# A hybrid decoder trunk on one core: GLA and HGRN2 level factors moved off GpSimd, HGRN2's diagonal computed as a score product, and a quarter's score products issued as one group

## The chip, the cores and the metric

The kernel runs on one core of one Trainium2 chip. The metric is device time in microseconds, lower is better. Before the change three runs gave 1830.06, 1832.36 and 1833.24 us, so the median is 1832.36 us.

## The reference, cut to what matters

One layer, 1024 tokens, model width 1024. The input is normalised and modulated, and one projection of 11416 columns (`w_in`) feeds four token mixers that work side by side: A (RWKV-7), B (GLA), C (mLSTM) and D (HGRN2). Their outputs are gated, projected again (`w_branch`), merged with sigmoid gates, passed through `w_out`, added to the input and normalised.

GLA and HGRN2 are the same recurrence. With q, k, a log decay per channel and v, in chunks:

```python
b = jnp.cumsum(gc, axis=2)
rel = jnp.where(causal[:, :, None], b[:, :, :, None, :] - b[:, :, None, :, :], -jnp.inf)
attn = jnp.einsum('bhik,bhjk,bhijk->bhij', qc, kc, jnp.exp(rel))
o = attn @ vc + jnp.einsum('bhik,bhkv->bhiv', qc * jnp.exp(b), state)
```

The exponent is the sum of the log decays between the key's token j and the query's token i. It is zero for j = i, so the diagonal of `attn` is the plain product of q and k of one token ("own key"). GLA has 4 heads of 64 key channels (two heads share 128 partitions: two "pairs"), HGRN2 4 heads of 128.

## The kernel before, in words

The work has four stretches. `make_u` forms the normalised input (to about 110 us). Pass A does the eight RWKV-7 heads (to about 700 us). The second pass runs eight units in the order d0, b0, d1, c0, d2, b1, d3, c1 (d is HGRN2, b is GLA, c is mLSTM), to about 1530 us. `merge` and `finish` do the rest.

Each unit is worked in four **quarters** of 256 tokens, two chunks of 128 each. `units` writes down: a quarter of this unit, then a share of the next unit's projections, then some projections of the merge gates (table `GB`). A projection (`project`, `mm3`, lines 314 to 316) splits fp32 weights into a high and a low part and does 24 matmuls of 128x512 per half of the tokens, into a `pj` bank. Its weights come by DMA into the one buffer `wraw` (SP queue), ScalarE casts them to `whi` (line 303), VectorE forms `wlo` (line 304).

The program text is not the order on the engines. The framework's planner fixes each engine's order when the kernel is built: among the instructions that are ready by its own cost estimates it takes the one of highest priority, which is the order of the text unless a block raises it. So the projections written behind a quarter fill the places on TensorE where that quarter's products would wait. On the chip each engine then follows its list strictly, and waits where an input is late.

A quarter of HGRN2 (`d_quarter`) or GLA (`b_quarter`) splits each chunk's causal matrix by **levels** s = 64, 32, 16, 8, 4, 2, 1 (`LV`): at level s a token in the right half of a block of 2s looks at the keys in the left half. `level_factor` gives for each level a tile `x` (tag `lx`) of exponentials of the distance to the middle of the block; VectorE multiplies its right halves by q (line 973) and its left halves by k (line 975), and TensorE multiplies the two (line 989 for HGRN2, line 1143 for GLA). For s = 32 to 2 the difference to the middle is taken on GpSimd (lines 860 and 865, tile `le`) and ScalarE takes the exponential (lines 862, 863 and 866). For s = 64 ScalarE does it alone (lines 855 and 856), with the middle as a bias column.

HGRN2's score products have 64 output rows, so they use half of TensorE's columns (128*64 in the profile); the two halves r = 1 and 0 alternate. There are 26 of them in a quarter, each recorded as two passes (52). Two more products (line 991) sum q times k, which GpSimd formed (`dg`, line 968), over the channels: the own-key terms. VectorE copies the valid blocks of the scores through masks (line 1000, COPY_PREDICATED) into `AT`, whose other places stay zero, and the own-key sums into `dq` (line 1001). TensorE forms `AT` by V plus `qe` by the state (lines 1006 and 1007) into a `yw` bank for each chunk, and VectorE adds `dq` times V and writes `O` to SBUF (line 1008). `rms_out` squares `O` on ScalarE (line 877), takes the root on GpSimd (lines 878 and 879), scales on VectorE (line 880), and its tail transposes the result through a `yw` bank and sends it to DRAM.

PSUM has two banks each for `pj`, `iv`, `sc` and `yw`. Two `AT` tiles serve HGRN2 and GLA in turn. SBUF tiles of a quarter come from a pool of 20 (`h260`).

```python
for li, s in enumerate(self.LV):
    for c in range(2):
        lhs = k if s == 1 else Z[li]
...
        for r in (1, 0) if s < 64 else (0,):
```

Of the kernel before, what the change touches and what calls it, by code (L numbers as in the profile page):

```python
# [9 lines left out]
F32 = mybir.dt.float32  # L10
F32R = mybir.dt.float32r
U32 = mybir.dt.uint32
# [6 lines left out]
P = 128  # L19
# [16 lines left out]
class Hybrid:  # L36
# [759 lines left out]
    def d_consts(self):  # L796
        nc, cp = self.nc, self.cp
        self.mres = {}
        for n in (32, 64, 128):
            m = cp.tile([P, QT], F32, name=f"mres{n}")  # L800
            nc.gpsimd.memset(m[:], 1.0)
            nc.gpsimd.memset(m[:, 0:QT:n], 0.0)
            self.mres[n] = m
        self.AT = []
        for b in range(2):
            t = cp.tile([P, 2, P], F32, name=f"AT{b}")
            nc.gpsimd.memset(t[:], 0.0)
            self.AT.append(t)
        self.atn = 0

        lb = self.prow["lb"]
        l = self.PT[:, lb : lb + 4]
        e = cp.tile([P, 4], F32, name="lbe")
        nc.vector.tensor_tensor(e[:], l, l, ALU.subtract)
        nc.scalar.activation(e[:], e[:], AF.Exp)
        r = cp.tile([P, 4], F32, name="lbr")
        nc.vector.reciprocal(r[:], e[:])
        nc.vector.tensor_tensor(e[:], e[:], r[:], ALU.mult)
        self.lb = cp.tile([P, 4], F32, name="lbt")
        nc.vector.tensor_tensor(self.lb[:], e[:], e[:], ALU.subtract)  # L820
        self.omlb = cp.tile([P, 4], F32, name="omlb")
        nc.vector.tensor_scalar(self.omlb[:], self.lb[:], -1.0, 1.0, ALU.mult, ALU.add)
# [18 lines left out]
    def level_factor(self, s, cs, lg):  # L841
# [10 lines left out]
        if s == 64:  # L852
# [4 lines left out]
            return x  # L857
        ref = sp(c)[:, :, 0, s - 1 : s].broadcast_to([P, nb, s])
        e = self.h("le")
        nc.gpsimd.tensor_tensor(sp(e)[:, :, 0, :], ref, sp(c)[:, :, 0, :], ALU.subtract)  # L860
        if s == 32:
            nc.scalar.activation(sp(x)[:, :, 0, :], sp(e)[:, :, 0, :], AF.Exp)
            nc.scalar.activation(sp(x)[:, :, 1, :], sp(c)[:, :, 1, :], AF.Exp)
        else:
            nc.gpsimd.tensor_tensor(sp(e)[:, :, 1, :], sp(c)[:, :, 1, :], ref, ALU.subtract)  # L865
            nc.scalar.activation(x[:, :QT], e[:, :QT], AF.Exp)  # L866
        return x
# [89 lines left out]
    def d_quarter(self, hd, qi, q, k, lg, v, sz, S):  # L957
# [8 lines left out]
        nc.vector.tensor_tensor(qe[:, :QT], qe[:, :QT], q, ALU.mult)  # L966
        dg = self.h("dg")
        nc.gpsimd.tensor_tensor(dg[:, :QT], q, k, ALU.mult)
        Z = []
# [8 lines left out]
        for c in range(2):  # L978
            cs_ = slice(c * P, (c + 1) * P)
            nc.tensor.matmul(ps_[:, cs_], lhsT=kT[:, cs_], rhs=V[:, cs_], start=True, stop=True)  # L980
        sc2 = [self.sc() for _ in range(2)]
        for li, s in enumerate(self.LV):
            for c in range(2):
                lhs = k if s == 1 else Z[li]
                rhs = Z[li][:, c * P : (c + 1) * P].rearrange("p (b z t) -> p b z t", z=2, t=s)[:, :, 1, :]

                for r in (1, 0) if s < 64 else (0,):
                    o = sc2[c][64 * r : 64 * r + 64, 64 * li : 64 * li + 64].rearrange("p (b t) -> p b t", t=s)
                    nc.tensor.matmul(o, lhsT=lhs[:, c * P + 64 * r : c * P + 64 * r + 64], rhs=rhs, start=True, stop=True)  # L989
        for c in range(2):  # L990
            nc.tensor.matmul(sc2[c][:, 448:449], lhsT=dg[:, c * P : (c + 1) * P], rhs=self.one[:], start=True, stop=True)
        AT = self.AT[self.atn % 2]
        self.atn += 1
        dq = self.sm.tile([P, 2], F32, tag="dq", bufs=4, name=self.nm("dq"))
        for c in range(2):
            for li, s in enumerate(self.LV):
# [3 lines left out]
                nc.vector.copy_predicated(o, m, sc2[c][pr, 64 * li : 64 * li + 64].rearrange("p (b t) -> p b t", t=s))  # L1000
            nc.vector.tensor_copy(dq[:, c : c + 1], sc2[c][:, 448:449])
        O = self.h("O")
        for c in range(2):
            cc = slice(c * P, (c + 1) * P)
            po = self.yw()
            nc.tensor.matmul(po[:, 0:P], lhsT=AT[:, c, :], rhs=V[:, cc], start=True, stop=False)
            nc.tensor.matmul(po[:, 0:P], lhsT=qe[:, cc], rhs=S[:], start=False, stop=True)
            nc.vector.scalar_tensor_tensor(O[:, cc], V[:, cc], dq[:, c : c + 1], po[:, 0:P], ALU.mult, ALU.add)
            Sn = self.sm.tile([P, P], F32, tag="dS", bufs=4, name=self.nm("dS"))
# [95 lines left out]
    def b_quarter(self, pr, qi, q, k, lg, v, sz):  # L1105
# [32 lines left out]
        for c in range(2):  # L1138
# [6 lines left out]
            nc.tensor.matmul(sc[1][:, 384:386], lhsT=dg[:, cc], rhs=self.bo2[:], start=True, stop=True)  # L1145
            AT = self.AT[self.atn % 2]
            self.atn += 1
            for li, s in enumerate(self.LV):
# [103 lines left out]
    def c_unit(self, pr):  # L1252
# [25 lines left out]
        def quarter(q):  # L1278
# [10 lines left out]
            c(C_MZ + 2 * pr * P, self.silu_ev("z0", R)), c(C_MZ + (2 * pr + 1) * P, self.silu_ev("z1", R)),  # L1289
        ], quarter  # L1290

    def units(self, names):
# [311 lines left out]
```

## Time and profile before

| | |
|---|---|
| median of 3 runs | 1832.36 us |
| the profiled execution | 1833.73 us, its span 1831.9 us |
| TensorE busy | 1729.2 us, 94% of the span |
| VectorE / ScalarE / GpSimd busy | 64% / 39% / 24% |
| granted TensorE clock, mean | 0.984 |

Busy time of TensorE counts overlapping matmuls once and includes the time in which a matmul only drains, so 94% does not say that it works at its peak. "PE" is TensorE's matmul, "PEld" its weight load, DVE is VectorE, ACT ScalarE, POOL GpSimd. In a group's line the numbers behind the first bar are the total busy time in us and the mean duration of one in ns; behind the second bar stands the idle time of the engine just before them, with what ended it.

### The profile page before, as it was taken

The numbers are of one execution on the slowest core, as the hardware profiler recorded it, in microseconds if no ns is written. First come the engines' busy times: TensorE is split into PE (matmuls) and PEld (weight loads), VectorE is DVE, ScalarE is ACT, GpSimd is POOL, SyncE is SP. The second block draws the span as 40 slices with busy tenths as digits, with TensorE's granted clock in tenths as the row PEclk, the third lists the DMA queues.
The fourth block names the chain that finished last, engine by engine and source line by source line (L and its number), as shares of the span: only waits on it lengthen the run. The fifth ranks groups of instructions, "written<-read, shape, count | busy, mean of one in ns | idle before, by whom it ended". The sixth has DMA issues, their size and how long they took to land. (4 is left out here: it accounts for less than half of the span.)

```text
span 1831.9 us, 28809 instructions
## 1 busy us (share of the span) xinstructions
PE 1729.2 (94%) x10515; PEld 1364.8 (75%) x10515; DVE 1179.8 (64%) x3125; ACT 719.4 (39%) x1612; POOL 438.1 (24%) x785
## 2 busy tenths in 40 slices
PE   5989999999999999999999999999989999999998
PEld 4766777777777777777677777777667788777786
DVE  8657867668667645666877545666887654565632
ACT  5643333333333356346333353536343343222221
POOL 4721121112111121121221202221231220175410
PEclk7989999999999999999999999999999999999999
DMA  9221222223222211111121221111112125666422
GB/s 299 56 68 42 54 81 56 55 65 77 49 68 56 70 49 47 58 52 44 50 58 53 64 57 53 59 53 38 56 35 66 43 82 176 208 202 203 150 85 81
DMA packets 224278, 147.30 MB, mean 80 GB/s; under 512 B 60511, under 2 KB 203018, under 8 KB 224138
## 3 DMA queue, kind: packets, MB, share of 16 engines
q1 hardware_dynamic: 208800, 109.23, 21.9%
q10 hardware_dynamic: 15338, 36.24, 5.6%
q8 instruction: 83, 1.36, 0.3%
q14 instruction: 57, 0.47, 0.1%
HBM read 111.88 MB, written 33.56 MB: 79 GB/s over the span
## 5 line engine op out<-in xcount | busy, mean ns | idle before, releaser
L314 PE MATMUL pj<-uh,whi 128*128 128x512 f32 x1344 | 548.0, 408 | 5.0 <-DVE rn L534 3.6
L316 PE MATMUL pj<-uh,wlo 128*128 128x512 f32 x1344 | 542.3, 404 | 0.0
L315 PE MATMUL pj<-ul,whi 128*128 128x512 f32 x1344 | 539.7, 402 | 0.0
L314 PEld LDWEIGHTS pj<-uh,whi 128*128 128x128 f32 x1344 | 254.8, 190 | 54.0 <-issue 7.0
L316 PEld LDWEIGHTS pj<-uh,wlo 128*128 128x128 f32 x1344 | 254.3, 189 | 49.1 <-issue 2.4
L315 PEld LDWEIGHTS pj<-ul,whi 128*128 128x128 f32 x1344 | 254.7, 190 | 45.6 <-issue 0.9
L303 ACT CAST whi<-wraw 128x1024 fp32r<-128x1024 f32 x89 | 93.0, 1045 | 235.3 <-PE pj L315 164.3
L304 DVE TENSOR_TENSOR wlo<-wraw,whi 128x1024 fp32r<-128x1024 f32 (+1 forms) x88 | 107.9, 1226 | 62.3 <-ACT whi L303 57.8
L860 POOL TENSOR_TENSOR le<-c 128x128 f32<-128x128 f32 x120 | 56.6, 480 | 266.5 <-DVE c L826 233.1
L670 DVE TENSOR_TENSOR tm<-nb,xr 32x1 f32<-32x1 f32 (+14 forms) x240 | 71.3, 297 | 6.2 <-DMA nb<-nd 0.5
L878 POOL TENSOR_SCALAR ss<-ss 128x2 f32<-128x2 f32 x48 | 15.6, 326 | 231.7 <-ACT on L877 229.9
L535 POOL TENSOR_TENSOR rn<-rn,nhalf 128x4 f32<-128x4 f32 x16 | 19.6, 1222 | 186.7 <-DVE rn L534 171.3
L1398 ACT ACTIVATE g<-pj 128x512 f32<-128x512 f32 x64 | 37.9, 593 | 64.7 <-PE pj L316 57.6
L887 DVE SCALAR_TENSOR_TENSOR y<-yw,DV,z 128x256 f32<-128x256 f32 x48 | 22.1, 480 | 57.7 <-PE yw L885 56.7
L1457 POOL TENSOR_TENSOR acc<-acc,g 128x512 f32<-128x512 f32 x32 | 46.8, 1477 | 50.2 <-DVE g L1455 50.2
L672 DVE TENSOR_REDUCE xr<-tm 32x1 f32<-32x1 f32 (+14 forms) x240 | 54.0, 225 | 6.5
L314 PE MATMUL iv<-yt,whi 128*128 128x512 f32 x128 | 50.4, 398 | 7.8 <-ACT yt L1410 4.8
L877 ACT ACTIVATE on<-O 128x128 f32<-128x128 f32 x64 | 19.8, 310 | 93.0 <-DVE O L1163 54.3
L745 DVE SCALAR_TENSOR_TENSOR Gbd<-Gbd,fa,yw 64x64 f32<-64x64 f32 x128 | 35.8, 279 | 27.9 <-PE yw L732 25.8
L989 PEld LDWEIGHTS sc<-lx 128*64 128x64 f32 x704 | 29.5, 137 | 30.9 <-issue 13.0
L314 PE MATMUL pj<-yt,whi 128*128 128x512 f32 x128 | 50.3, 393 | 1.8 <-DVE g L1455 1.8
L866 ACT ACTIVATE lx<-le 128x256 f32<-128x256 f32 x96 | 39.7, 416 | 28.1 <-POOL le L865 27.9
(482 smaller groups left out, 3564.3 us busy)
## 6 DMA issues: line engine op xcount, KB each, us to landing
wraw<-in_w_in_dram SPq DMA_DIRECT2D x89, 512.0 KB
gdram<-g ACTq DMA_DIRECT2D x64, 256.0 KB
th<-gdram ACTq DMA_DIRECT2D x32, 512.0 KB
adaw<-in_ada_w_dram SPq DMA_DIRECT2D x16, 512.0 KB
ydram<-y SPq DMA_DIRECT2D x64, 128.0 KB
wraw<-in_w_branch_dram SPq DMA_DIRECT2D x16, 512.0 KB
yr<-ydram SPq DMA_DIRECT2D x32, 256.0 KB
x<-in_x_dram SPq DMA_DIRECT2D x8, 512.0 KB
```

Of the source, the lines that this page charges most:

```text
L303: nc.scalar.copy(hi[:, :nk, :width], raw[:, :nk, :width])
L304: eng.tensor_tensor(lo[:, :nk, :width], raw[:, :nk, :width], hi[:, :nk, :width].bitcast(F32), ALU.subtract)
L314: nc.tensor.matmul(ps[:width, :], lhsT=a, rhs=xh[:, k, :], start=k == 0, stop=False)
L315: nc.tensor.matmul(ps[:width, :], lhsT=a, rhs=xl[:, k, :], start=False, stop=False)
L316: nc.tensor.matmul(ps[:width, :], lhsT=b, rhs=xh[:, k, :], start=False, stop=k == nk - 1)
L670: nc.vector.tensor_tensor(t2, n2[:, 0:i, i].unsqueeze(1).broadcast_to([32, i, i]), x2[:, 0:i, 0:i].rearrange("p j l -> p l j"), ALU.mult)
L672: nc.vector.reduce_sum(x2[:, i, 0:i], t2, axis=AX.X)
L745: nc.vector.scalar_tensor_tensor(Gn[hr, hr], Gc[hr, hr], fa[hr, c : c + 1], yw[hr, P + 64 * h : P + 64 * h + 64], ALU.mult, ALU.add)
L860: nc.gpsimd.tensor_tensor(sp(e)[:, :, 0, :], ref, sp(c)[:, :, 0, :], ALU.subtract)
L866: nc.scalar.activation(x[:, :QT], e[:, :QT], AF.Exp)
L1398: nc.scalar.activation(g[:], ps[:], AF.Tanh, scale=0.5)
L1457: nc.gpsimd.tensor_tensor(a, a, g[:], ALU.add)
```

## The change

1. `level_factor`, used by GLA and HGRN2 (24 quarters): for s = 32 ScalarE takes four exponentials of 32 columns with the middle as bias, and one of the right halves; for s = 16 to 2 VectorE subtracts the middle from all 256 columns, and ScalarE takes the absolute value and then the exponential of its negative. GpSimd has no part in it any more.
2. `d_quarter`: `dg`, its two products and `dq` go. Instead k by q is formed as a 128x128 product for each chunk into a `yw` bank (`pd`), and VectorE copies its diagonal through the identity as a mask into `AT`. As the own-key terms are then inside `AT`, the sum for `O` is complete in PSUM; both chunks go into one `yw` bank, which `rms_out` reads.
3. The 26 score products go to a new helper `together`: it raises their priority, issues the first one (now s = 1, the levels are in reverse order), and puts the others behind it in TensorE's order.
4. HGRN2 and GLA get an `AT` pair each.

```diff
@@ -801,11 +801,13 @@
             nc.gpsimd.memset(m[:], 1.0)
             nc.gpsimd.memset(m[:, 0:QT:n], 0.0)
             self.mres[n] = m
-        self.AT = []
-        for b in range(2):
-            t = cp.tile([P, 2, P], F32, name=f"AT{b}")
-            nc.gpsimd.memset(t[:], 0.0)
-            self.AT.append(t)
+        self.AT = {}
+        for u in "db":
+            self.AT[u] = []
+            for b in range(2):
+                t = cp.tile([P, 2, P], F32, name=f"AT{u}{b}")
+                nc.gpsimd.memset(t[:], 0.0)
+                self.AT[u].append(t)
         self.atn = 0
 
         lb = self.prow["lb"]
@@ -855,15 +857,17 @@
                 nc.scalar.activation(x[:, o : o + s], c[:, o : o + s], AF.Exp, scale=-1.0, bias=c[:, o + s - 1 : o + s])
             nc.scalar.activation(sp(x)[:, :, 1, :], sp(c)[:, :, 1, :], AF.Exp)
             return x
-        ref = sp(c)[:, :, 0, s - 1 : s].broadcast_to([P, nb, s])
-        e = self.h("le")
-        nc.gpsimd.tensor_tensor(sp(e)[:, :, 0, :], ref, sp(c)[:, :, 0, :], ALU.subtract)
         if s == 32:
-            nc.scalar.activation(sp(x)[:, :, 0, :], sp(e)[:, :, 0, :], AF.Exp)
+            for b in range(nb):
+                o = 2 * s * b
+                nc.scalar.activation(x[:, o : o + s], c[:, o : o + s], AF.Exp, scale=-1.0, bias=c[:, o + s - 1 : o + s])
             nc.scalar.activation(sp(x)[:, :, 1, :], sp(c)[:, :, 1, :], AF.Exp)
-        else:
-            nc.gpsimd.tensor_tensor(sp(e)[:, :, 1, :], sp(c)[:, :, 1, :], ref, ALU.subtract)
-            nc.scalar.activation(x[:, :QT], e[:, :QT], AF.Exp)
+            return x
+
+        blk = lambda t: t[:, :QT].rearrange("p (b t) -> p b t", t=2 * s)
+        nc.vector.tensor_tensor(blk(x), blk(c), blk(c)[:, :, s - 1 : s].broadcast_to([P, nb, 2 * s]), ALU.subtract)
+        nc.scalar.activation(x[:, :QT], x[:, :QT], AF.Abs)
+        nc.scalar.activation(x[:, :QT], x[:, :QT], AF.Exp, scale=-1.0)
         return x
 
     def rms_out(self, m, q, ct, O, sz, g, eps):
@@ -964,8 +968,6 @@
         qe = self.h("qe")
         nc.scalar.activation(qe[:, :QT], c128[:, :QT], AF.Exp)
         nc.vector.tensor_tensor(qe[:, :QT], qe[:, :QT], q, ALU.mult)
-        dg = self.h("dg")
-        nc.gpsimd.tensor_tensor(dg[:, :QT], q, k, ALU.mult)
         Z = []
         for s in self.LV:
             x = self.level_factor(s, cs, lg)
@@ -978,34 +980,37 @@
         for c in range(2):
             cs_ = slice(c * P, (c + 1) * P)
             nc.tensor.matmul(ps_[:, cs_], lhsT=kT[:, cs_], rhs=V[:, cs_], start=True, stop=True)
+
+        pd = self.yw()
+        for c in range(2):
+            cs_ = slice(c * P, (c + 1) * P)
+            nc.tensor.matmul(pd[:, cs_], lhsT=k[:, cs_], rhs=q[:, cs_], start=True, stop=True)
         sc2 = [self.sc() for _ in range(2)]
-        for li, s in enumerate(self.LV):
-            for c in range(2):
-                lhs = k if s == 1 else Z[li]
-                rhs = Z[li][:, c * P : (c + 1) * P].rearrange("p (b z t) -> p b z t", z=2, t=s)[:, :, 1, :]
-
-                for r in (1, 0) if s < 64 else (0,):
-                    o = sc2[c][64 * r : 64 * r + 64, 64 * li : 64 * li + 64].rearrange("p (b t) -> p b t", t=s)
-                    nc.tensor.matmul(o, lhsT=lhs[:, c * P + 64 * r : c * P + 64 * r + 64], rhs=rhs, start=True, stop=True)
-        for c in range(2):
-            nc.tensor.matmul(sc2[c][:, 448:449], lhsT=dg[:, c * P : (c + 1) * P], rhs=self.one[:], start=True, stop=True)
-        AT = self.AT[self.atn % 2]
+
+        def level(li, s, c, r):
+            lhs = k if s == 1 else Z[li]
+            rhs = Z[li][:, c * P : (c + 1) * P].rearrange("p (b z t) -> p b z t", z=2, t=s)[:, :, 1, :]
+            o = sc2[c][64 * r : 64 * r + 64, 64 * li : 64 * li + 64].rearrange("p (b t) -> p b t", t=s)
+            return nc.tensor.matmul(o, lhsT=lhs[:, c * P + 64 * r : c * P + 64 * r + 64], rhs=rhs, start=True, stop=True)
+
+
+        todo = [(li, s, c, r) for li, s in reversed(list(enumerate(self.LV))) for c in range(2) for r in ((1, 0) if s < 64 else (0,))]
+        self.together([lambda t=t: level(*t) for t in todo])
+        AT = self.AT["d"][self.atn % 2]
         self.atn += 1
-        dq = self.sm.tile([P, 2], F32, tag="dq", bufs=4, name=self.nm("dq"))
+        nc.vector.copy_predicated(AT[:], self.ident[:].bitcast(U32).unsqueeze(1).broadcast_to([P, 2, P]),
+                                  pd[:, 0:QT].rearrange("p (c t) -> p c t", t=P))
         for c in range(2):
             for li, s in enumerate(self.LV):
                 pr = slice(0, P if s < 64 else 64)
                 o = AT[pr, c, :].rearrange("p (b z t) -> p b z t", z=2, t=s)[:, :, 1, :]
                 m = self.pmL[s][pr].bitcast(U32).rearrange("p (b t) -> p b t", t=s)
                 nc.vector.copy_predicated(o, m, sc2[c][pr, 64 * li : 64 * li + 64].rearrange("p (b t) -> p b t", t=s))
-            nc.vector.tensor_copy(dq[:, c : c + 1], sc2[c][:, 448:449])
-        O = self.h("O")
+        O = self.yw()
         for c in range(2):
             cc = slice(c * P, (c + 1) * P)
-            po = self.yw()
-            nc.tensor.matmul(po[:, 0:P], lhsT=AT[:, c, :], rhs=V[:, cc], start=True, stop=False)
-            nc.tensor.matmul(po[:, 0:P], lhsT=qe[:, cc], rhs=S[:], start=False, stop=True)
-            nc.vector.scalar_tensor_tensor(O[:, cc], V[:, cc], dq[:, c : c + 1], po[:, 0:P], ALU.mult, ALU.add)
+            nc.tensor.matmul(O[:, cc], lhsT=AT[:, c, :], rhs=V[:, cc], start=True, stop=False)
+            nc.tensor.matmul(O[:, cc], lhsT=qe[:, cc], rhs=S[:], start=False, stop=True)
             Sn = self.sm.tile([P, P], F32, tag="dS", bufs=4, name=self.nm("dS"))
             nc.vector.scalar_tensor_tensor(Sn[:], S[:], f[:, c : c + 1], ps_[:, cc], ALU.mult, ALU.add)
             S = Sn
@@ -1143,8 +1148,7 @@
                 nc.tensor.matmul(sc[li // 4][:, P * (li % 4) : P * (li % 4) + P], lhsT=lhs,
                                  rhs=R[li][:, c].rearrange("p h t -> p (h t)"), start=True, stop=True)
             nc.tensor.matmul(sc[1][:, 384:386], lhsT=dg[:, cc], rhs=self.bo2[:], start=True, stop=True)
-            AT = self.AT[self.atn % 2]
-            self.atn += 1
+            AT = self.AT["b"][c]
             for li, s in enumerate(self.LV):
                 o = AT[:].rearrange("p c (b z t) -> p c b z t", z=2, t=s)[:, :, :, 1, :]
                 m = self.pmL[s][:].bitcast(U32).rearrange("p (b t) -> p b t", t=s).unsqueeze(1).broadcast_to([P, 2, 64 // s, s])
@@ -1288,6 +1292,14 @@
             c(C_MV + 2 * pr * P, self.qcopy("v0", R)), c(C_MV + (2 * pr + 1) * P, self.qcopy("v1", R)),
             c(C_MZ + 2 * pr * P, self.silu_ev("z0", R)), c(C_MZ + (2 * pr + 1) * P, self.silu_ev("z1", R)),
         ], quarter
+
+    def together(self, fs):
+
+        with self.tc.high_priority():
+            first = fs[0]()
+            with self.tc.issue_after(first.ins):
+                for f in fs[1:]:
+                    f()
 
     def units(self, names):
```

## Rows read from the trace of the kernel before

**Rows 1.** The profile page: its first line.

```profile
span 1831.9 us, 28809 instructions
```

**Rows 2.** A stretch: us, busy PE, PEld, DVE, ACT, POOL (x), PEclk, DMA share, GB/s.

```profile
700.00:1530.00 830.00, 784.65 (x4511) 620.78 (x4510) 552.34 (x1576) 354.85 (x906) 179.26 (x364) 0.99 0.19 55
```

**Rows 3.** TensorE's timeline in the last HGRN2 quarter: start, us, engine, line, tiles, count, idle.

```profile
1438.17 0.39 PE L316 MATMUL pj<-uh,wlo 128*128 128x512 f32 x1
...
1439.89 0.49 PE L314 MATMUL pj<-uh,whi 128*128 128x512 f32 x1
...
1441.66 0.51 PE L315 MATMUL pj<-ul,whi 128*128 128x512 f32 x1
...
1442.95 0.61 PE L991 MATMUL sc<-one,dg 128*128 128x1 f32 x4
1443.41 0.48 PE L316 MATMUL pj<-uh,wlo 128*128 128x512 f32 x1
1443.73 0.39 PE L314 MATMUL pj<-uh,whi 128*128 128x512 f32 x1
1443.96 0.40 PE L315 MATMUL pj<-ul,whi 128*128 128x512 f32 x1
```

**Rows 4.** The same timeline in the second HGRN2 quarter.

```profile
757.41 0.50 PE L315 MATMUL pj<-ul,whi 128*128 128x512 f32 x1
757.85 0.69 PE L989 MATMUL sc<-lx 128*64 128x64 f32 x16
758.46 0.50 PE L316 MATMUL pj<-uh,wlo 128*128 128x512 f32 x1
```

**Rows 5.** TensorE's groups, 700 to 1530 us: count | busy, mean ns | idle before.

```profile
L989 PE MATMUL sc<-lx 128*64 128x64 f32 x704 | 39.4, 231 | 9.7 <-DVE lx L975 8.0 <-ACT lx L866 0.3
L1143 PE MATMUL sc<-Zr,lx 128*128 128x128 f32 x192 | 35.3, 293 | 8.1 <-DVE lx L1134 6.3
```

**Rows 6.** GpSimd's groups, 700 to 1530 us.

```profile
L860 POOL TENSOR_TENSOR le<-c 128x128 f32<-128x128 f32 x120 | 56.6, 480 | 266.5 <-DVE c L826 233.1 <-PE iv L917 15.5 <-issue 14.1
L865 POOL TENSOR_TENSOR le<-c 128x128 f32<-128x128 f32 x96 | 47.4, 494 | 0.0
```

**Rows 7.** VectorE's timeline in the last HGRN2 quarter: start, us, instruction.

```profile
1438.94 0.51 DVE L975 TENSOR_TENSOR lx<-lx,dk 128x128 f32<-128x128 f32 x1
1439.38 0.48 DVE L973 TENSOR_TENSOR lx<-lx,q 128x128 f32<-128x128 f32 x1
...
1441.26 0.28 DVE L975 TENSOR_TENSOR lx<-lx,dk 128x128 f32<-128x128 f32 x1
1441.47 0.30 DVE L973 TENSOR_TENSOR lx<-lx,q 128x128 f32<-128x128 f32 x1
...
1449.24 0.43 DVE L880 TENSOR_TENSOR on<-O,ss 128x256 f32<-128x256 f32 x1 [1.53 <-POOL ss L879]
```

**Rows 8.** VectorE's groups from 700 to 1530 us.

```profile
L973 DVE TENSOR_TENSOR lx<-lx,q 128x128 f32<-128x128 f32 x112 | 41.6, 372 | 2.2 <-ACT lx L866 2.1
L975 DVE TENSOR_TENSOR lx<-lx,dk 128x128 f32<-128x128 f32 x96 | 38.7, 403 | 0.0
...
L1152 DVE COPY_PREDICATED AT<-pmL,sc 128x128 f32<-128x128 uint32 x112 | 36.3, 337 | 3.0 <-PE sc L1145 0.9
...
L1008 DVE SCALAR_TENSOR_TENSOR O<-V,dq,yw 128x128 f32<-128x128 f32 x32 | 11.1, 348 | 19.1 <-PE yw L1007 17.5
...
L838 DVE TENSOR_TENSOR kt<-kt,dk 128x256 f32<-128x256 f32 x16 | 6.8, 422 | 3.7 <-ACT kt L835 3.5
```

**Rows 9.** ScalarE's groups, 700 to 1530 us.

```profile
L866 ACT ACTIVATE lx<-le 128x256 f32<-128x256 f32 x96 | 39.7, 416 | 28.1 <-POOL le L865 27.9
...
L855 ACT ACTIVATE lx<-c 128x64 f32<-128x64 f32 x48 | 13.8, 338 | 0.6 <-DVE c L826 0.6
```

**Rows 10.** The waits view of the whole span: total us, times, longest us.

```profile
ACT whi L303 <- PE pj L315: 164.3, 54, 5.6
```

**Rows 11.** The weight loads from 700 to 1530 us.

```profile
L989 PEld LDWEIGHTS sc<-lx 128*64 128x64 f32 x704 | 29.5, 137 | 30.9 <-issue 13.0 <-DVE lx L975 7.0 <-ACT lx L863 4.8
```

## The prediction

> **What bounds the kernel now.** The first line of the page gives the span, 1831.9 us [rows 1]. I then cut the span into stretches. Every line that the change touches runs in the second pass, 700 to 1530 us, and there TensorE is busy 784.65 of 830 us, while VectorE has 552, ScalarE 355 and GpSimd 179 us of work [rows 2]. TensorE's order is fixed when the kernel is built, so the end moves by what a stretch of that order gets shorter or longer, and work of another engine counts only where TensorE waits for it. The later stretches follow behind in the same order, so a microsecond won here should reach the end.
>
> Busy time hides how well TensorE is used, so I went to its timeline. Projection matmuls follow each other every 0.23 us, although each is shown 0.39 to 0.40 us long (1443.73 to 1443.96) [rows 3]: what an item costs TensorE is the distance to the next start, not its duration. In the last HGRN2 quarter the score products lie in pieces among projections. From 1438.17 to 1443.73 are 5.56 us, in which four projection matmuls start [rows 3]. They are worth 4 x 0.23 = 0.92, so the scores with the two own-key products cost 4.64 us. Read in this way the sixteen quarters cost 3.1 to 4.8 us, 4.4 on average (of them the last one's rows are shown), 70 us in all.
>
> **Tying the score products together.** A piece in the second quarter shows the price without any wait: from 757.41 to 758.46 there is one projection matmul and 16 passes, 1.05 - 0.23 = 0.82 us [rows 4]. The 16 passes span 0.69 us and one takes 0.23 on average [rows 5], so they start (0.69 - 0.23) / 15 = 0.031 us apart and need 0.47. The remaining 0.35 is the change from 128*128 to 128*64 and back, and the projection after it is late by another 0.32 - 0.23 = 0.09, as at 1443.41 [rows 3]. So a piece pays 0.44 us besides its passes. One run of 52 passes should cost 51 x 0.031 + 0.44 = 2.0 us.
>
> The own-key part: the old products take 0.46 us (1442.95 to 1443.41) [rows 3]. In place of four passes of one column there are four of 128 columns, in the form of the projections. Bounds: nothing more than now, or four whole durations of the nearest row, 4 x 0.293 = 1.17 us [rows 5], which is 0.7 a quarter and 11 us in all. I take 0.5, since matmuls of one form overlap as the projections do. That makes 2.5 us a quarter without a wait, against 4.4: a gain of 1.9 x 16 = 30 us.
>
> Now the wait. The run starts with the factor that is made last (s = 1), so it waits once for everything. Today all pieces together wait 9.7 us, 0.6 a quarter, nearly all for line 975 [rows 5]. Bounds for the new wait: nothing, or today's 0.6 plus what the chain of factors gets longer (next part, 1 us), 1.6. I take 0.6, the measured one, since it is the same engine and the same lag behind the planner's order. The gain becomes (4.4 - 2.5 - 0.6) x 16 = 21 us. Behind the waiting run stand only the projections of the next unit, and ScalarE's and VectorE's copies of them; no DMA is moved, and the SP and GpSimd queues keep their order.
>
> **The level factors.** GpSimd loses lines 860 and 865, 56.6 + 47.4 = 104 us, and HGRN2's q times k [rows 6]. It is no bound, so this by itself is worth nothing, but it had a side effect. While GpSimd subtracts, VectorE's multiplications take 0.48 to 0.51 us and start 0.44 apart; afterwards, in the same quarter, 0.28 to 0.30 and 0.21 apart [rows 7]. Lines 973 and 975 average 372 and 403 ns [rows 8]; at 280 that frees (0.092 x 112) + (0.123 x 96) = 22 us of VectorE in the HGRN2 quarters alone.
>
> VectorE gets 4 subtractions of 256 columns in each of 24 quarters. The nearest row is line 838, 422 ns [rows 8]: 96 x 0.42 = 41 us. The O additions go, 11.1 us, and `dq`; a masked copy of 256 columns comes in each HGRN2 quarter, bounded by one and two of line 1152's 337 ns [rows 8], 5 to 11 us. Sum for VectorE: about 41 - 22 - 11 + 8 = +16 us before GLA's share of the relief, on 552 of 830. It is no bound on average.
>
> ScalarE gets 96 absolute values at 416 ns, 40 us, and for s = 32 four short exponentials in place of one; the nearest row is 338 ns for 64 columns [rows 9], so 24 x 3 x 0.34 = 24 us more. Its 355 become about 420 of 830: hidden, as long as the planner has projections to put in front of a quarter's products.
>
> What isn't hidden by busy shares is the length of the chain in a quarter. Before, a level took two GpSimd steps, some 0.84 us, as VectorE's pairs show (1438.94 to 1439.38 is one of two steps) [rows 7]. After it a level takes two ScalarE steps of 0.42 [rows 9], of which the second needs the first: the same 0.84. For s = 32 three short activations more, 1 us at most, delay the last factor. In GLA, where products stay in pieces, 8 quarters pay up to 1 us each, or win back up to their present wait for factors, 8.1 us [rows 5]. Between +8 and -8 I take nothing.
>
> **O in PSUM.** One `yw` bank is held until line 880 is done, which starts 1.53 us after VectorE is free for it and takes 0.43 [rows 7], so some 2 us longer than before. Price: nothing if the planner has another matmul, up to 2 x 16 = 32 us if TensorE stood still for it each time. I take nothing, since the projections use other banks. The separate `AT` pairs and the memsets at the start of the pass lie beside other work: nothing.
>
> **The sum.** -21 us on the profiled execution's 1833.73 us is 1812.7. That execution stands 1.4 us over the median, so against the median the forecast is 1811.4, given as 1811.
>
> **The rivals.**
> The waits vanish altogether (chance 0.18). GpSimd no longer slows the factors, so the run finds them ready, and GLA's waits go as well: 1832.4 - 30 - 8 = 1794. For it: the waits are for line 975, whose 403 ns lie halfway between the quick and the slow form [rows 7, 8]. Against it: ScalarE now carries each level twice.
>
> The wait takes the place of the pieces (0.22). The chain now passes ScalarE twice in each level, and ScalarE is one queue: the cast of the next weights stands in it and waits for projections to free its buffer, 164.3 us over the span and up to 5.6 us at a time [rows 10]. If the cast stands ahead of a factor, the whole run waits, where before only one piece did. At 1.9 us of wait a quarter the gain is gone, 1832; at 3 us it costs 1.1 x 16 = 18 us, 1850. Against it: the planner puts the run where its own estimate has the factors ready, and today's waits per piece are short. I give 0.08 to a gain of less than 10 us, and 0.14 to the decisive form, slower than before.
>
> The run is not one run (0.05). Only the first product is held in front; if in the planner's order s = 1 is ready before the others, these follow when they are ready, with projections between. Then only VectorE's relief is left: at most the present waits, 10 us, so 1822 to 1832.
>
> The run takes as long as its pieces (0.02). If the weight loads of neighbouring products did not overlap their matmuls, each pass would cost its load too: 29.5 us over 704 loads is 42 ns [rows 11], so 52 x (42 + 31) = 3.8, and with 0.44 and 0.5 4.7 us a quarter: no gain, 1834. Rows 4 speak against it, as its 0.031 us a pass have the loads in them. This is a rule of the Trainium skill (TensorE: Matmul & The Clock Gate, section "Part 3: Packing small matmuls"): a weight load overlaps with running matmuls only where the row group differs, and all these products use all rows. The trace does not agree, with 16 passes in 0.69 us.
>
> **How the numbers follow.** The forecast, 1804 to 1822, has 0.53, the better case 0.18, the shared waits 0.22, the broken run 0.05, the page's rule 0.02. About 0.2% (3.7 us) is what a measurement of this kernel can tell from no change. Faster by more: 0.53 + 0.18 and most of 0.08 and 0.05 from the small gains, minus some for a planner's order that comes out otherwise in GLA: 0.77. Within: 0.09. Slower: 0.14. The range goes from 1794, the better case, to 1834, where the gain is eaten up; beyond it lies the decisive wait.
>
> **What would show it.** Right: line 989 in one row of 52 passes in each quarter, some 1.6 us long, with one wait of VectorE or ScalarE in front that is under 1 us; lines 973 and 975 near 280 ns; GpSimd's 179 us in the second pass under 80; the second pass some 20 us shorter. Wrong: a wait over 1.9 us ahead of each run, score products still in pieces, TensorE idle for a `yw` bank, or GLA's products waiting for ScalarE by much more than 8.1 us.

## The result and the profile after

The changed kernel takes 1799.29 us (median of 4 runs, 1795.84 to 1800.49) against 1831.21 us of the kernel before in the same comparison (4 runs, 1829.36 to 1833.24). The ratio is 0.982, with a 95% interval from 0.980 to 0.984: 32 us faster, where 21 were forecast. The profiled execution took 1800.29 us, its span is 1798.1.

The first line of the changed kernel's page answers to [rows 1]:

```profile
span 1798.1 us, 28703 instructions
```

The windows view of the changed kernel has the columns of [rows 2]. Its first line answers to [rows 2]; the second is the place where a GLA quarter begins and is used further down.

```profile
700.00:1530.00 830.00, 799.77 (x4653) 646.99 (x4652) 541.47 (x1638) 398.74 (x1090) 69.15 (x134) 0.98 0.22 64
...
860.00:870.00 10.00, 6.32 (x26) 4.40 (x25) 7.18 (x18) 5.23 (x19) 0.00 (x0) 0.78 0.51 144
```

In the same 830 us TensorE now starts 4653 matmuls where it started 4511: the second pass gets through sooner. GpSimd falls from 179 to 69 us. ScalarE rises by 44 us, and VectorE, for which I had forecast 16 us more, has 11 less. The granted clock of the stretch is a little lower, 0.98 against 0.99.

TensorE's timeline in the last HGRN2 quarter of the changed kernel answers to [rows 3]:

```profile
1411.19 0.39 PE L314 MATMUL pj<-uh,whi 128*128 128x512 f32 x1
1411.51 0.46 PE L994 MATMUL sc<-lx,dk 128*64 128x64 f32 x8
1411.80 1.57 PE L994 MATMUL sc<-lx 128*64 128x64 f32 x44
1413.30 0.50 PE L315 MATMUL pj<-ul,whi 128*128 128x512 f32 x1
1413.64 0.39 PE L316 MATMUL pj<-uh,wlo 128*128 128x512 f32 x1
```

The 52 passes are one run, with no wait in front. From 1411.19 to 1413.64 are 2.45 us, and two projection matmuls start in it, worth 2 x 0.23. So the run costs 1.99 us; the forecast was 2.0. Fourteen of the sixteen quarters come out at 1.98 or 1.99 in the same way, the other two at 3.3 and 5.7.

TensorE's groups from 700 to 1530 us answer to [rows 5]:

```profile
L1148 PE MATMUL sc<-Zr,lx 128*128 128x128 f32 x192 | 35.0, 292 | 1.1 <-DVE lx L1139 0.4
L994 PE MATMUL sc<-lx 128*64 128x64 f32 x704 | 25.2, 222 | 0.1
L921 PE MATMUL iv<-ident,kt 128*128 128x128 f32 x48 | 9.7, 283 | 9.3 <-DVE kt L840 8.9
L994 PE MATMUL sc<-lx,dk 128*64 128x64 f32 x128 | 7.3, 233 | 2.0 <-DVE lx L975 2.0
L1125 PE MATMUL iv<-V,kT 128*64 128x128 f32 x64 | 6.2, 322 | 4.3 <-ACT kT L926 4.3
```

The wait ahead of the sixteen runs is 2.0 us altogether, 0.13 a quarter. GLA's products (line 1143 before, now 1148) waited 8.1 us [rows 5] and wait 1.1. What is late now comes earlier in a quarter: the transposes of the decayed keys (`kt`, line 921; the result is `kT`) wait 9.3 us for VectorE, where they waited 7.7. This is their line in the kernel before:

```profile
L917 PE MATMUL iv<-ident,kt 128*128 128x128 f32 x48 | 9.8, 285 | 7.7 <-DVE kt L838 6.9
```

Summed over all of TensorE's groups of this stretch, the waits are 45.4 us before and 30.3 after.

VectorE's groups of the same stretch answer to [rows 8]:

```profile
L868 DVE TENSOR_TENSOR lx<-c 128x256 f32<-128x256 f32 x96 | 36.3, 418 | 0.2
L975 DVE TENSOR_TENSOR lx<-lx,q 128x128 f32<-128x128 f32 x112 | 31.7, 284 | 0.4 <-ACT lx L870 0.4
L977 DVE TENSOR_TENSOR lx<-lx,dk 128x128 f32<-128x128 f32 x96 | 27.1, 283 | 0.0
...
L1001 DVE COPY_PREDICATED ATd<-ident,yw 128x256 f32<-128x256 uint32 x16 | 6.9, 430 | 4.8 <-PE yw L987 4.8
```

The multiplications by q and k (973 and 975 before, now 975 and 977) take 284 and 283 ns; the forecast was 280. The new subtraction takes 418 ns, forecast 0.42 us.

### The profile page after: what moved, and what is told of

Read it like the earlier page. It is cut to its first block, busy times and chain, and to the rows that moved or that the text cites. A ratio compares the mean times of both kernels' runs of the same rounds, so it can differ in the third digit from the quotient of the medians.

```text
span 1798.1 us, 28703 instructions
## 1 busy us (share of the span) xinstructions
PE 1710.5 (95%) x10515; PEld 1363.1 (76%) x10515; DVE 1161.5 (65%) x3173; ACT 753.7 (42%) x1780; POOL 325.9 (18%) x555
## 4 chain that ended last, share of the span: by engine, by line
PE 72%; DVE 13%; ACT 5%; DMA 3%; POOL 3%; issue 3%; SPq 0%; POOLq 0%; ACTq 0%; DVEq 0%
PE pj L314 15%; PE pj L316 15%; PE pj L315 14%; PE yw L732 3%; PE sc L683 3%; DMA wraw<-in_w_in_dram 2%; PE iv L315 2%; PE iv L316 2%; PE iv L314 2%; DVE adacc L229 1%; PE sc L994 1%; DVE tm L670 1%; PE sc L1148 1%; PE sc L620 1%; PE iv L921 1%
## 5 line engine op out<-in xcount | busy, mean ns | idle before, releaser
L315 PEld LDWEIGHTS pj<-ul,whi 128*128 128x128 f32 x1344 | 255.5, 190 | 45.4 <-issue 1.0
L314 PE MATMUL iv<-yt,whi 128*128 128x512 f32 x128 | 50.4, 397 | 6.8 <-ACT yt L1422 5.2
L314 PE MATMUL pj<-yt,whi 128*128 128x512 f32 x128 | 50.4, 394 | 1.8 <-DVE g L1467 1.8
L315 PE MATMUL iv<-yt,whi 128*128 128x512 f32 x128 | 50.1, 393 | 0.5 <-DVE yt L1423 0.5
L316 PE MATMUL pj<-yt,wlo 128*128 128x512 f32 x128 | 50.0, 390 | 0.6 <-DVE wlo L1435 0.6
L315 PE MATMUL pj<-yt,whi 128*128 128x512 f32 x128 | 50.0, 390 | 0.0
L316 PE MATMUL iv<-yt,wlo 128*128 128x512 f32 x128 | 49.7, 390 | 0.0
```

What stands on the lines that cost most here:

```text
L314: nc.tensor.matmul(ps[:width, :], lhsT=a, rhs=xh[:, k, :], start=k == 0, stop=False)
L315: nc.tensor.matmul(ps[:width, :], lhsT=a, rhs=xl[:, k, :], start=False, stop=False)
L316: nc.tensor.matmul(ps[:width, :], lhsT=b, rhs=xh[:, k, :], start=False, stop=k == nk - 1)
```

## The experiments

T stands for tying the score products, D for the level factors without GpSimd, K for the own-key part with `O` in PSUM and the separate `AT` pairs, which always come with it here. Ratios are to the kernel before, with 95% intervals.

**Each part alone.**

e1_tie: the kernel before with T only.

```diff
-for li, s in enumerate(self.LV):
-    for c in range(2):
...
+todo = [... for li, s in reversed(list(enumerate(self.LV))) ...]
+self.together([lambda t=t: level(*t) for t in todo])
```

> Only the run: HGRN2's score products are tied and in reverse order; decays stay on GpSimd, own-key products stay as they were behind the run. Theory S (what counts is the changes of form, 0.44 us a piece): 4.4 falls to 2.0 + 0.46 + the wait. With a wait of 0.6 us per run the gain is 21 us, about 1810. Rival C (the waits are made by GpSimd slowing VectorE, and they stay as long as GpSimd subtracts): the run waits 0.6 to 1.0 us, gain 14 to 21. Rival P (the planner puts a tied run only where its factors are ready, so tying removes the waits too): line 989 waits under 2 us in all, gain about 30, 1801.

1825.29 us, ratio 0.996 (0.995 to 0.998): 5 us, less than any of the theories gave. TensorE's timeline in the last quarter, and its group from 700 to 1530 us:

```profile
1431.44 0.46 PE L986 MATMUL sc<-lx,dk 128*64 128x64 f32 x8 [1.63 <-DVE lx L973]
1431.72 1.57 PE L986 MATMUL sc<-lx 128*64 128x64 f32 x44
...
L986 PE MATMUL sc<-lx,dk 128*64 128x64 f32 x128 | 7.3, 233 | 19.3 <-DVE lx L973 19.1
```

The run is in one piece and as short as in the full change, but it waits for its last factor, 19.3 us in all, 1.2 a quarter.

e2_decay: the kernel before with the new `level_factor` only.

```diff
-nc.gpsimd.tensor_tensor(sp(e)[:, :, 0, :], ref, sp(c)[:, :, 0, :], ALU.subtract)
...
+nc.vector.tensor_tensor(blk(x), blk(c), blk(c)[:, :, s - 1 : s].broadcast_to([P, nb, 2 * s]), ALU.subtract)
+nc.scalar.activation(x[:, :QT], x[:, :QT], AF.Abs)
+nc.scalar.activation(x[:, :QT], x[:, :QT], AF.Exp, scale=-1.0)
```

> Only the new level factors; products stay in pieces, own-key part as before. Theory S: the pieces stay, so nothing is gained but waits; rival C: with VectorE's multiplications at 280 ns the waits of lines 989 and 1143 (9.7 and 8.1 us) go to under 3 us together, gain 10 to 18 us, about 1817. Rival P: the waits stay near 18 us and the time within 5 us of before.

1825.9 us, ratio 0.998 (0.997 to 0.999). TensorE's groups:

```profile
L991 PE MATMUL sc<-lx 128*64 128x64 f32 x704 | 37.6, 230 | 1.4 <-DVE lx L977 1.2
L1145 PE MATMUL sc<-Zr,lx 128*128 128x128 f32 x192 | 34.6, 289 | 1.1 <-DVE lx L1136 0.4
L919 PE MATMUL iv<-ident,kt 128*128 128x128 f32 x48 | 9.8, 287 | 12.0 <-DVE kt L838 11.5
```

Score waits fall from 9.7 and 8.1 us [rows 5] to 1.4 and 1.1, some 15 us, and 4 us arrive. Part of it turned into other waits: `kt` 7.7 to 12.0, and the products with `kT` 5.0 to 7.1, so that all waits of TensorE together fall from 45.4 to 38.3. The products are still in pieces.

e3_ownkey: the kernel before with K only (old factors, old loop).

```diff
-nc.gpsimd.tensor_tensor(dg[:, :QT], q, k, ALU.mult)
...
+nc.tensor.matmul(pd[:, cs_], lhsT=k[:, cs_], rhs=q[:, cs_], start=True, stop=True)
...
+O = self.yw()
```

> Only the own-key part as score diagonals, with O left in PSUM; pieces and GpSimd decays as before. All theories: the two products cost as much as the two that they replace, within 0.2 us a quarter, so within 4 us of before. If holding the bank for O costs, TensorE waits for it and the time is 5 us or more longer.

1823.54 us, ratio 0.996 (0.995 to 0.998). I had priced this part at nothing. TensorE's groups:

```profile
L919 PE MATMUL iv<-ident,kt 128*128 128x128 f32 x48 | 9.7, 284 | 6.5 <-DVE kt L840 6.1
L985 PE MATMUL yw<-q,dk 128*128 128x128 f32 x64 | 10.7, 292 | 0.5 <-DVE y L889 0.5
```

The products of k and q wait for nothing that counts, so holding a `yw` bank longer cost next to nothing (0.5 us). The waits for `kt` and for its transposed copy `kT` fall, 7.7 to 6.5 and 5.0 to 2.4.

**The change without one part.** e4_no_decay has the GpSimd lines back (T and K), e5_no_tie the old loop of score products (D and K), e6_no_ownkey the old own-key sums and shared `AT` tiles (T and D). Against the changed kernel:

```diff
-nc.vector.tensor_tensor(blk(x), blk(c), ...)                     e4_no_decay
+nc.gpsimd.tensor_tensor(sp(e)[:, :, 0, :], ref, ...)
...
-self.together([lambda t=t: level(*t) for t in todo])             e5_no_tie
+for li, s in enumerate(self.LV):
...
-nc.tensor.matmul(pd[:, cs_], lhsT=k[:, cs_], rhs=q[:, cs_], ...)  e6_no_ownkey
+nc.gpsimd.tensor_tensor(dg[:, :QT], q, k, ALU.mult)
```

> The change without the new level factors: run and own-key part stay, GpSimd subtracts again. Theory S: the run still costs 2.0 us, so most of the gain stays, 20 us or more of 32. Rival C: VectorE's multiplications are back at 480 ns in contact with GpSimd, the waits ahead of the run and in GLA come back, and 10 to 18 us of the 32 are lost, about 1812.

> The change without the run: products in the old order and in pieces, new level factors and own-key part stay. Theory S: 16 quarters pay their pieces again, 2 to 4 changes of form of 0.44 us more than one run, 14 to 28 us slower than the changed kernel, 1814 to 1827. Rival C: only the waits mattered, so it is within 8 us of the changed kernel.

> The change without the own-key part: q times k on GpSimd and its two products behind the run, O through VectorE to SBUF; run and new level factors stay. The own-key part is priced at nothing: within 4 us of the changed kernel, 1795 to 1804. If it carried a hidden gain (one form change less, VectorE's additions), the time is 5 to 10 us longer.

| | median us | ratio | interval |
|---|---|---|---|
| e4_no_decay (T, K) | 1817.03 | 0.993 | 0.991 to 0.994 |
| e5_no_tie (D, K) | 1816.04 | 0.992 | 0.991 to 0.993 |
| e6_no_ownkey (T, D) | 1807.12 | 0.987 | 0.986 to 0.988 |
| full change | 1799.29 | 0.982 | 0.980 to 0.984 |

TensorE's groups, first of e4_no_decay, then of e5_no_tie, then of e6_no_ownkey:

```profile
L992 PE MATMUL sc<-lx,dk 128*64 128x64 f32 x128 | 7.3, 233 | 20.7 <-DVE lx L973 20.7
```

```profile
L997 PE MATMUL sc<-lx 128*64 128x64 f32 x704 | 37.0, 230 | 1.1 <-DVE lx L977 0.9 <-DVE lx L975 0.2
```

```profile
L988 PE MATMUL sc<-lx,dk 128*64 128x64 f32 x128 | 7.3, 233 | 2.5 <-DVE lx L975 2.5
L919 PE MATMUL iv<-ident,kt 128*128 128x128 f32 x48 | 9.9, 287 | 11.8 <-DVE kt L838 11.2
```

T and D need each other. T brings 0.4% on the kernel before and, with D in place, 1.1% (e6_no_ownkey against e2_decay) or 1.0% (the full change against e5_no_tie). With the old factors the run waits 19 to 21 us, with the new ones 2.0 to 2.5. K is worth 0.4 to 0.6% beside every combination, 7 to 10 us. T and D without K (e6_no_ownkey) gain 23 us.

**Is it GpSimd's load or the shape of the new chain?** e7_ghost is the changed kernel, with GpSimd's old subtractions done as well, into a tile that nobody reads. The computation is unchanged; the tile takes buffers of the `h260` pool, too.

```diff
+g_ = self.h("gh")
+nc.gpsimd.tensor_tensor(sp(g_)[:, :, 0, :], gref, sp(c)[:, :, 0, :], ALU.subtract)
+if s < 32:
+    nc.gpsimd.tensor_tensor(sp(g_)[:, :, 1, :], sp(c)[:, :, 1, :], gref, ALU.subtract)
```

> The changed kernel, with GpSimd doing its old subtractions into a tile that nothing reads: the result is the same, only VectorE's neighbour is busy again. Rival C: lines 973 and 975 go back towards 400 ns, waits come back ahead of the run and in GLA, 5 to 18 us slower than the changed kernel. Theory S and P: under 4 us slower.

1831.12 us, ratio 1.000 (0.999 to 1.001): the whole gain is gone, more than the 18 us that I had given at most. VectorE's and TensorE's groups:

```profile
L873 DVE TENSOR_TENSOR lx<-c 128x256 f32<-128x256 f32 x96 | 47.7, 534 | 0.2
L980 DVE TENSOR_TENSOR lx<-lx,q 128x128 f32<-128x128 f32 x112 | 36.9, 330 | 0.4 <-ACT lx L875 0.4
L999 PE MATMUL sc<-lx,dk 128*64 128x64 f32 x128 | 7.3, 233 | 22.4 <-DVE lx L980 22.4
L1153 PE MATMUL sc<-Zr,lx 128*128 128x128 f32 x192 | 35.1, 292 | 7.1 <-DVE Zr L1141 4.4 <-DVE lx L1144 1.5 <-ACT v L912 0.6
```

The subtraction goes from 418 to 534 ns, the multiplication from 284 to 330, and the runs wait 22.4 us again. That GpSimd's work brings the wait ahead of the runs back, and with it the old time, is shown: all of TensorE's waits together go from 30.3 to 58.3 us. The planner's order is not the cause. By the two traces TensorE and ScalarE have the same instructions in the same order, and VectorE too, but for one memset that changes places with its neighbour. The pool's buffers can be read from the waits, first of e7_ghost, then of the changed kernel, from 700 to 1530 us:

```profile
ACT lx L874 <- DVE lx L873: 28.1, 45, 2.0
...
ACT lx L874 <- POOL gh L864: 0.9, 1, 0.9
...
ACT lx L869 <- DVE lx L868: 7.1, 14, 1.4
```

ScalarE waits longer for VectorE's subtractions. Only one wait of another engine, 0.9 us, ends with a subtraction that nobody reads, and none of VectorE or ScalarE for a level's tile ends with TensorE giving a buffer free. So the trace shows the slower VectorE as the way, and next to nothing by the pool. The Trainium skill (SBUF — State Buffer, section "Who interferes with whom") says that VectorE and GpSimd share one pair of ports under an exclusive lock. The longer subtraction agrees with it; no price for a whole kernel is given there, and here it is 32 us.

**Does the order inside the run matter?** e9_forward is the changed kernel with the levels from 64 down to 1, so that the product ready first is issued first.

```diff
-todo = [... for li, s in reversed(list(enumerate(self.LV))) for c in range(2) ...]
+todo = [... for li, s in enumerate(self.LV) for c in range(2) ...]
```

> The changed kernel with the levels in their first order inside the tied group, so that the first product is s = 64, whose factor is made first, and the others may follow one by one as the planner has them ready. If it is the late first product that keeps the group whole, the products of line 994 fall into pieces again and the time goes towards the kernel without the run, 1816. If raised priority alone keeps them together, it is within 4 us of the changed kernel, 1795 to 1804.

1815.83 us, ratio 0.991 (0.990 to 0.993), the time of e5_no_tie. TensorE's timeline in the last quarter:

```profile
1424.14 0.45 PE L994 MATMUL sc<-lx 128*64 128x64 f32 x4
...
1425.42 0.45 PE L994 MATMUL sc<-lx 128*64 128x64 f32 x8
...
1426.92 0.69 PE L994 MATMUL sc<-lx 128*64 128x64 f32 x16
...
1428.20 0.69 PE L994 MATMUL sc<-lx 128*64 128x64 f32 x16
1428.72 0.41 PE L994 MATMUL sc<-lx,dk 128*64 128x64 f32 x8
```

Four pieces again, 3.04 us in this quarter, where the run costs 1.99. `together` ties nothing by itself: it holds only because its first product is the last to be ready.

**GLA.** e8_gla_tied issues GLA's seven products of a chunk through `together`; e11_gla_old gives GLA alone its GpSimd factors back (`True` chooses the old branch, in `b_quarter`).

```diff
-for li, s in enumerate(self.LV):
-    lhs = (k if s == 1 else Z[li])[:, cc]
...
+self.together([lambda t=t: glevel(*t) for t in reversed(list(enumerate(self.LV)))])
```

> The changed kernel with GLA's 7 score products of each chunk tied in the same way. They have the form of the projections, 128*128, so by theory S no change of form is saved: within 4 us of the changed kernel. If pieces of any kind cost (fp32 products among rounded ones), line 1148's marginal cost of some 150 ns a pass falls towards 110: 224 x 0.04 = 9 us faster, about 1790.

```diff
-x = self.level_factor(s, cs, lg)
+x = self.level_factor(s, cs, lg, True)
```

> The changed kernel with the old level factors in GLA alone (8 of 24 quarters); HGRN2 keeps the new ones. If the new factors help by taking GpSimd off VectorE in each mixer for itself, GLA's score waits (1.1 us) go back to about 8, the ones ahead of HGRN2's runs stay near 2, and the time is 5 to 10 us longer than the changed kernel, 1804 to 1810. If only HGRN2's relief counts, it is within 3 us.

e8_gla_tied: 1799.61 us, ratio 0.983 (0.982 to 0.984), no different from the change. Its groups on TensorE:

```profile
L1148 PE MATMUL sc<-Zr,lx 128*128 128x128 f32 x192 | 26.1, 276 | 1.0 <-DVE lx L1139 1.0
L1148 PE MATMUL sc<-Zr,k 128*128 128x128 f32 x32 | 7.1, 304 | 8.9 <-DVE Zr L1136 5.2 <-DVE ATb L1158 3.8
L994 PE MATMUL sc<-lx,dk 128*64 128x64 f32 x128 | 7.7, 242 | 9.3 <-DVE lx L975 9.3
```

The products take 26.1 us of TensorE in place of 35.0, and what that saves is given back as waits of 8.9 and 9.3 us: TensorE's waits together rise from 30.3 to 37.6 us.

e11_gla_old: 1796.36 us, ratio 0.981 (0.979 to 0.982). That is 3 us less than the change by the medians, with intervals that overlap: GLA's new factors earn nothing. Its groups on TensorE and its window at the place shown for the change:

```profile
L1159 PE MATMUL sc<-Zr,lx 128*128 128x128 f32 x192 | 35.4, 293 | 8.1 <-DVE lx L1150 6.2
L932 PE MATMUL iv<-ident,kt 128*128 128x128 f32 x48 | 9.7, 284 | 6.6 <-DVE kt L840 6.1
...
860.00:870.00 10.00, 8.30 (x44) 5.78 (x45) 9.03 (x27) 4.67 (x14) 4.59 (x9) 1.00 0.20 54
```

The wait of 8.1 us is back, but `kt` waits 6.6 instead of 9.3, `kT` 2.2 instead of 4.3. In these 10 us, in which a GLA quarter begins, TensorE is busy for 8.30 us at clock 1.00, where the changed kernel has 6.32 at 0.78.

**Taking the next wait away.** e10_kt_late is the changed kernel with the `kt` transposes and the state products, which only the end of a quarter needs, behind the score products, in HGRN2 and GLA (in GLA behind those of the first chunk). e12_late_gla_old adds GLA's old factors.

```diff
-f, kT = self.carried(c128, k)
+f, kt = self.carried(c128, k)
...
+first = self.together([lambda t=t: level(*t) for t in todo])
+with self.tc.issue_after(first.ins):
+    kT = self.turn(kt, "kT")
```

> The changed kernel, with the transposes of the carried keys (line 921, kt) and the state products behind them put after the score products in TensorE's order, in GLA and HGRN2. They are the longest waits left in the second pass: 9.3 us before the transposes and 4.3 before GLA's state products, and the clock falls to half behind some of them. If these waits go and nothing takes their place: 8 to 14 us faster than the changed kernel, about 1788. If the next item in the order waits instead (the copies into AT, the state of the second chunk): within 4 us of it, or slower.

> Both last edits in one kernel: the carried keys' transposes and state products behind the score products, and the old level factors in GLA. If the two gains are separate (waits for the carried keys; the clock in GLA's stretches, which ran at half rate less with the old factors), the time is about 1796 - 9 = 1787, under each of them. If both win by the same thing, the clock and the waits at the quarters' start, it is 1790 to 1796 again.

e10_kt_late: 1790.47 us, ratio 0.978 (0.977 to 0.980), the fastest kernel of this study by the median. TensorE's groups:

```profile
L921 PE MATMUL iv<-ident,kt 128*128 128x128 f32 x48 | 10.5, 298 | 0.0
L1153 PE MATMUL iv<-V,kT 128*64 128x128 f32 x64 | 5.3, 285 | 0.0
L989 PE MATMUL sc<-lx,dk 128*64 128x64 f32 x128 | 7.3, 233 | 6.1 <-DVE lx L975 5.9
```

The waits for `kt` and `kT`, 13.6 us, are gone; 4.1 us come back ahead of the runs, and GLA's products with the state now wait 7.2 us for `qe`. The projections wait 6.2 us for ScalarE, where they waited 0.1. All of TensorE's waits together are 29.9 us, as long as in the changed kernel (30.3). By the medians the end is 9 us earlier than there, by the profiled spans 4.3 (1793.8 against 1798.1; the profiled execution, 1795.89 us, is this kernel's slowest). What brought this gain, the traces don't show.

e12_late_gla_old: 1808.68 us, ratio 0.988 (0.986 to 0.990), a miss: two edits of which neither cost anything alone are together 18 us slower than e10_kt_late. Its edit is the two diffs of e10_kt_late and e11_gla_old. TensorE's groups:

```profile
L1177 PE MATMUL yw<-Sbd,qe 128*128 128x256 f32 x32 | 10.6, 413 | 10.7 <-DVE qe L1131 10.7
L1155 PE MATMUL sc<-Zr,lx 128*128 128x128 f32 x192 | 38.5, 313 | 8.4 <-DVE lx L1146 4.2 <-DVE Zr L1143 3.3
```

GLA's products wait 8.4 us, where e10_kt_late has 2.3, and the products with the state 10.7 for `qe`, where it has 7.2. All of TensorE's waits together rise from 29.9 to 37.8 us, and the time at half clock (last section) from 27.2 to 37.4, by an estimate worth 5.1. Together that is 13.0 us, about the 12.7 between the two profiled spans (1793.8 and 1806.5). Why the two edits bring these waits only together stays open.

## Why the prediction was right, and where its sizes were off

**The sum.** Read by distances between starts, the sixteen quarters' scores cost 70.3 us before and 36.9 after, where 9.1 us of own-key products stand apart: a gain of 24.3 us. GLA's score products, from end to end, went from 43.5 to 33.6 us, 9.9 less. Together that is 34.2 of the 33.8 us by which the profiled spans differ, so the other lines cancel out. The forecast had 21 and 0. That T and D alone come to 23 us, close to the 21, is partly luck. Read in the same way, e6_no_ownkey gains 24.3 us at HGRN2's scores and 9.9 at GLA's, and loses again by what the sum didn't have: longer waits for `kt` and `kT` (12.7 to 18.6 us) and more time at half clock (13.6 to 20.4 us, last section).

**The pieces: right.** 2.0 us a run was forecast from one piece of the second quarter, and 1.99 measured. The two odd quarters have the run's only waits, 0.9 and 1.1 us, and in the second of them the products with V wait another 2.2 us for `ATd` right behind the run.

**The wait ahead of the run: the term that failed.** I took 0.6 us, today's wait, "since it is the same engine and the same lag behind the planner's order". It measured 0.13, which is 0.47 x 16 = 7.5 us more gain. Some 4 of them are lost again, 1.1 in own-key products and the rest in the two odd quarters, which leaves the 24.3 - 21 = 3 us by which the scores beat the forecast. It wasn't the same lag: e1_tie shows 1.2 us with GpSimd in the chain, and the full change 0.13 without. The lag was GpSimd's, which slowed VectorE and stood in the chain itself; the same change took it away. I had the evidence (0.48 to 0.51 us against 0.28 to 0.30 [rows 7]), used it for VectorE's sum and for the better rival, and left the wait of the sum as it was. The rival in which the waits vanish, 1794 at chance 0.18, is what happened in mechanism; it had no own-key part, and no waits for `kt` or loss of clock.

**The level's chain: mis-sized.** I held two ScalarE steps that need each other for the same 0.84 us as before. ScalarE's timeline of the changed kernel:

```profile
1408.01 0.73 ACT L869 ACTIVATE lx<-lx 128x256 f32<-128x256 f32 x2
1408.64 0.71 ACT L870 ACTIVATE lx<-lx 128x256 f32<-128x256 f32 x2
1409.25 0.71 ACT L869 ACTIVATE lx<-lx 128x256 f32<-128x256 f32 x2
1409.87 0.71 ACT L870 ACTIVATE lx<-lx 128x256 f32<-128x256 f32 x2
```

The planner takes two absolute values, then two exponentials. So two levels pass in 1409.25 - 1408.01 = 1.24 us, 0.62 for one: while one level's second step waits for its first, the other level's first step runs. ScalarE's busy time, forecast at about 420 us, is 399.

**VectorE: 11 us less, where I had 16 more.** By line, from the second pass on, the subtractions add 40.1 us and the masked copy 6.9, and `O` and HGRN2's multiplications take 11.1 and 21.5 away: so far the forecast's terms. Not in it were GLA's multiplications, 8.1 us less, line 880, which reads PSUM in HGRN2 now, 7.9 less (0.42 to 0.43 us in all sixteen quarters, where thirteen took some 0.95 before), and `dq`, 5.3 less. The rest lies in smaller lines.

**The own-key part: priced at nothing, worth 7 to 10 us.** On TensorE the price was right (8.6 us before, 9.1 after, end to end), and holding `O` in a bank cost next to nothing (0.5 us of waits for a `yw` bank in e3_ownkey). What I left out is that VectorE, 552 us busy before and 534 with K alone, loses this work at the end of a quarter, where the next one's `kt` is due: the additions for `O`, 11.1 us [rows 8], and the parts of line 880 and `dq` named above, less the masked copy. The waits for `kt` and `kT` together are 12.7 us before, 8.9 with K alone, 19.1 with D alone, 18.6 with T and D, and 13.6 with all three: D makes the start of a quarter late, and K takes 4 to 5 us of that back. That it does so by VectorE's work is argued from these waits; no run shows it by itself. K also takes the product of q and k, 11.6 us, off GpSimd and separates the `AT` pairs, and no run has these apart. The pairs can hardly count: all named waits of VectorE's copies into `AT` were for score products before (10.7 and 0.9 us), none for a free `AT`. The rest of the 7 to 10 us stays open.

**GLA: taken at nothing, between 8 us either way.** By the sum above its products gave 9.9 us, and their waits fell by 7.0. But e11_gla_old, without this gain, is no slower than the change (3 us faster by the medians). So it did not reach the end: by the traces it came back as waits for `kt` and `kT`, 4.8 us more than there, and as time at half clock (last section). Nothing was the right value for the end and the wrong one for the line.

**The other rivals.** The wait takes the place of the pieces: that is e1_tie and e4_no_decay, 1.2 to 1.3 us a quarter, under the 1.9 at which the gain would have been gone. But the cause was GpSimd, not a weight cast on ScalarE. The run is not one run: excluded by the timeline, and e9_forward shows how near it was. The run takes as long as its pieces: 44 passes in 1.57 us. A rule of the Trainium skill (TensorE: Matmul & The Clock Gate, section "Part 3: Packing small matmuls") would have made each pass pay its weight load; the trace does not agree here either.

## What to carry to other kernels

Where small products with a costly entry lie in pieces, tie them into one run, and put the one that is ready last at its head; but the run then waits once for the slowest chain, so shorten that chain in the same change: here either edit alone gave under 0.5%, and both with the third 1.8%. A GpSimd operation that is far from being the bound can still set the pace of VectorE, and a copy of it with no reader is a cheap way to see its price. A wait that disappears from one group is only won when no other group has it: read the waits of all of TensorE's lines and add them up, not those of the line that was changed.

## What the runs showed that I had not expected

The granted clock takes part in the sum. The mean over the runs was 0.986 for the kernel before, 0.983 for the changed one and 0.987 for e11_gla_old. It goes with GLA's new factors: the kernels that have them lie at 0.983 or 0.984 (e7_ghost at 0.980), those with the old ones at 0.986 or 0.987, but for e12_late_gla_old, 0.980. In the changed kernel's trace TensorE was granted half its rate (1.2 instead of 2.4 GHz) for 27.2 us between 700 and 1530 us, before for 13.6. Two of the stretches, 6.8 us each, lie at the second quarter of a GLA unit, where TensorE had waited 1.4 to 1.5 us for `kt` and 2.1 to 2.2 for `kT`. In the first of them, from 867.61 to 869.31, projections start 0.42 to 0.43 us apart in place of 0.23. In e11_gla_old, whose TensorE waits less there, both are gone, and 6.8 us are left in all. If half-rate time costs half of itself, the change gave back (27.2 - 13.6) / 2 = 6.8 us in this way; that is an estimate from these numbers. The means over the runs give 0.003 of 1800 us, 5 us. So a gain in waits can be returned by the clock. That the waits at the quarter's start are the cause is argued, not shown: e10_kt_late has neither these waits nor these two stretches, but 27.2 us at half rate in other places, and e4_no_decay waits 20.7 us ahead of its runs and has 6.8. Single executions of one kernel differ, too (0.981 to 0.985 for the changed one).

The second surprise is e7_ghost: GpSimd is busy 166 us between 700 and 1500 us there and 68 in the changed kernel, and these 98 us of work, whose results nobody reads, take all of the 32 us.
